# A two-layer hybrid trunk: the gate chain laid out on 32 rows, and retention tiles normalised in pairs

## The chip, the cores and the metric

The kernel runs on one core of a Trainium2 chip. The metric is the device time of one execution in microseconds (us); smaller is better. The kernel before was timed three times: 2268.85, 2267.9 and 2268.21 us, median 2268.21 us. A further execution was profiled: it took 2268.18 us, of which the recorded span of instructions is 2266.5 us.

## What is computed

Two layers run one after the other on x (1024 tokens by 1024 columns, f32). Each normalises x with gain and shift from a conditioning vector, multiplies by a wide input matrix, and cuts the result into two groups of four heads of 256 columns. The mLSTM heads have a short causal convolution, gates and a running maximum; the retention heads have rotary tables and a fixed decay. Both end in a per-head normalisation, a gate and an output product.

The part that the change touches first is the gate arithmetic of the mLSTM. Per head and token there are an input gate value `li` and a forget value `lf`:

```python
lf = log_sigmoid(f_pre)              # min(f, 0) - ln(1 + exp(-|f|))
b  = cumsum(lf)                      # over the tokens
u  = li - b
m  = running_max(u)                  # m0 = 0
# later: exp(u - m), exp(m_end - m), exp(-(b + m)), per token and head
```

The reference does it in chunks of 64; the kernel does it once over all 1024 tokens of 4 heads. Sums are kept in two pieces, a coarse one rounded to a grid (`bq`, from `lfq`) and a remainder (`br`), so that differences stay exact enough.

The second part is the retention group's per-head normalisation: for each tile of 128 tokens by 256 columns, subtract the mean and divide by the root of the variance plus a constant that depends on the place of the tile in its chunk.

## The kernel before, in words

**Matmuls.** Every f32 product is made of three matmuls of a high and a low half of each operand (`mm3`, lines 177 to 179, written `L177` to `L179` in the profile). A projection of one column block by 512 tokens is 24 such matmuls. Most projections are done in groups of seven products instead of eight (`pair_product` for q, k and z columns, `vpair_product` for the values of two heads), which costs additions on VectorE: of the token matrix once per layer (`build_forms`, L626 to L648) and of each weight block (`total`, L705).

**Order.** TensorE's order is the program's own (`tc.manual_schedule(engines={PE})`): a matmul that waits holds all matmuls behind it. The other engines' order is chosen by a planner that simulates the program; what is wrapped in `late(...)`, or called through the class `Later`, is pinned behind the instruction that was written just before it on its engine. All queues are in order on the chip, SyncE's (SP, which issues most DMAs) too.

**Ticks.** The side work is written as generators. `launch(gen, delay)` starts one, and `yield n` lets n ticks pass. A tick follows each unit of TensorE work: a quarter of a projection (12 matmuls of 128x512), or a slot. In the value products a slot is 24 matmuls of 128x256; a pair of heads takes 14 slots, in the order a12, a11, S2, S1, S3, a22, S4, two slots each. They write two kinds of PSUM tile: a12 pz, a11 px, S2 px, S1 pz, S3 px, a22 px, S4 pz. a22 adds to the bank that S3 wrote, so it has to wait until VectorE has read S3 (L824).

**The gate chain** (`gate_chain`, L503 to L590) is launched once per layer, when `gate_units` (L495) has put the gates of 1024 tokens into two PSUM tiles `pgs`, 4 rows of forget values (0 to 3) and 4 of input values (32 to 35), 512 tokens each. Around it run `build_forms` (in both layers), `rotary_tables` (layer 0 only) and the loading of the adaLN rows (`ada_rows`, L299, L307 and L309, and in layer 1 `gate_rows` with its product L345). The chain's own steps, for two halves of 512 tokens on 4 rows:

- tick 1: five ScalarE activations for each half (L516 to L519, L524)
- ticks 13 to 17, and 18 to 22 for the second half: fifteen VectorE instructions each, on 4 rows of 512, among them three scans (running sums and a running maximum, L535, L536, L548) that go on from the half before; four of them write into a 128-row tile `T4`. As V is `Later()`, the profile shows all of them as L144.
- tick 26: eight TensorE transposes of 128x128 (L562) turn the two `T4` into columns by token, copied to `COL`; then the exponentials for all heads. In layer 1, L345 follows on TensorE.

The chain's running maximum also goes to DRAM (`mdr`, L553), from where the attention reads it as rows. As working space the chain uses buffers that the attention owns later (`q`, `kc`, `dm`, `nd`, `cf`, `n`, `zt`, `cH`, `cL`).

**Retention normalisation.** `attention` runs per head by a table of steps. `values(j, tts)` makes the output tiles `tts` of chunk j; for retention heads it copies each to `nrm[j]` (one buffer, `n`) with L1144. Chunk 0 makes both tiles in one step; chunks 1 to 3 make them in two steps, some ticks apart, and each step launches a `normalise` of its own: statistics (L1160, L1161), variance plus constant (L1174), a power of minus one half on GpSimd (L1175, which writes `rsd`), minus mean times that (L1178, `nmu`), and the scaling on ScalarE (L1180). After the second tile, `finish` transposes the pair into `zt` (L1188) and stores it. That frees the buffer `n`.

Of the kernel before, what the change touches and what calls it, by code (L numbers as in the profile page):

```python
# [19 lines left out]
P = 128  # L20
# [67 lines left out]
def tile_hybrid_trunk(ctx, tc, x, xt, c, positions, w_ada, b_ada, norm_g, w_in, w_blk, w_val, conv_w, conv_b,  # L88
# [23 lines left out]
    def wt(tag, n, bufs, dt=F32):  # L112
        t = wrk.tile([P, 516 if tag == "acc" else n], dt, tag=tag, bufs=bufs, name=nm(tag))
        return t[:, 0:n] if tag == "acc" else t
# [91 lines left out]
           for l in range(DEPTH)]  # L206
    gbd = [dpool.tile([P, HALF], F32, name=f"gbd{i}") for i in range(2)]
    mdr = [dpool.tile([NH, T], F32, name=f"mdr{l}") for l in range(DEPTH)]

    ring = [cst.tile([P, 4 * 258], F32R, tag=f"ring{i}", name=f"ring{i}") for i in range(2)]  # L210
    ring3 = [r.rearrange("p (a c) -> p a c", a=4) for r in ring]
# [291 lines left out]
    def gate_chain(l, pgs, gt):  # L503
        V = Later()
        bg = cols[l][1]
        COL = wt("COL", 8 * 16, 1)
        C4 = COL.rearrange("p (t k h) -> p t k h", t=8, k=4)
        prev = {}
        on4 = ones.to_broadcast([P, 512])
        lfs, lis_, es = [], [], []  # L510
        mxs, fbs, lif = wt("q", 1024, 2), wt("q", 1024, 2), wt("kc", 1024, 1)
        for half in range(2):
            pg = pgs[half]
            hs = slice(half * HALF, (half + 1) * HALF)
            fb, li, e = fbs[:, hs], lif[:, hs], wt("dm", 512, 2)
            A.activation(fb[0:4], pg[0:4, :], AF.Identity, bias=bg[0:4, :])  # L516
            A.activation(li[32:36], pg[32:36, :], AF.Identity, bias=bg[32:36, :])
            A.activation(e[0:4], fb[0:4], AF.Abs)
            A.activation(e[0:4], e[0:4], AF.Exp, scale=-1.0)  # L519
            lfs.append(fb)  # L520
            lis_.append(li)
            es.append(e)
        for half in range(2):
            A.activation(es[half][0:4], es[half][0:4], AF.Ln, bias=ones[0:4, 0:1])  # L524
        yield 12
        T4s = []
        for half in range(2):
            lf, li, e = lfs[half], lis_[half], es[half]
            lfq = (wt("cf", 516, 1) if half else wt("nd", 516, 1))[:, 0:512]
            V.scalar_tensor_tensor(lf[0:4], lf[0:4], 0.0, e[0:4], ALU.min, ALU.subtract)  # L530
            V.tensor_scalar(lfq[0:4], lf[0:4], MAG_Q, -MAG_Q, ALU.add, ALU.add)
            V.tensor_tensor(lf[0:4], lf[0:4], lfq[0:4], ALU.subtract)
            bq, br = e, wt("zt", 512, 1) if half else wt("n", 512, 1)
            yield 1
            V.tensor_tensor_scan(bq[0:4], on4[0:4], lfq[0:4], prev.get("bq", 0.0), ALU.mult, ALU.add)  # L535
            V.tensor_tensor_scan(br[0:4], on4[0:4], lf[0:4], prev.get("br", 0.0), ALU.mult, ALU.add)  # L536
            yield 1
            lir, T4, mx = li, wt("cL" if half else "cH", 516, 1)[:, 0:512], mxs[:, half * HALF:(half + 1) * HALF]
            liq, uh = lf, lfq
            V.tensor_scalar(liq[0:4], li[32:36], MAG_Q, -MAG_Q, ALU.add, ALU.add)  # L540
            V.tensor_copy(lir[0:4], li[32:36])
            V.tensor_tensor(lir[0:4], lir[0:4], liq[0:4], ALU.subtract)
            G.memset(T4, 0.0)
            V.tensor_tensor(uh[0:4], liq[0:4], bq[0:4], ALU.subtract)
            yield 1
            V.tensor_copy(T4[0:4], uh[0:4])
            V.tensor_tensor(T4[32:36], lir[0:4], br[0:4], ALU.subtract)
            V.tensor_tensor_scan(mx[0:4], on4[0:4], uh[0:4], prev.get("mx", 0.0), ALU.mult, ALU.max)  # L548
            yield 1
            V.tensor_copy(T4[64:68], mx[0:4])  # L550
            V.tensor_tensor(uh[0:4], bq[0:4], mx[0:4], ALU.add)
            V.tensor_tensor(T4[96:100], uh[0:4], br[0:4], ALU.add)
            Q.dma_start(mdr[l][:, half * HALF:(half + 1) * HALF], mx[0:4])  # L553
            prev = {"bq": bq[0:4, 511:512], "br": br[0:4, 511:512], "mx": mx[0:4, 511:512]}
            T4s.append(T4)
            yield 1
        yield 3
        for half in range(2):
            T4 = T4s[half]
            pt = ps_a()  # L560
            for i in range(4):
                PE.transpose(pt[:, i * P:(i + 1) * P], T4[:, i * P:(i + 1) * P], ident)  # L562
            V.tensor_copy(C4[:, half * 4:(half + 1) * 4],
                          pt.rearrange("p (t k h) -> p t k h", t=4, k=4)[:, :, :, 0:4])
# [24 lines left out]
        V.tensor_tensor(we, we, eul4[:, :, 0:6, 0], ALU.mult)  # L589
        gt.update(C4=C4, eul4=eul4, em3=em3, wi=wi, we=we, dc=dc)  # L590
# [386 lines left out]
    def attention(l, hg, gt):  # L977
# [120 lines left out]
        def values(j, tts):  # L1098
# [6 lines left out]
            src = {}  # L1105
# [10 lines left out]
            for tt in tts:  # L1116
# [20 lines left out]
                if ml:  # L1137
                    if j > 0:
                        launch(gather(nd3[:, tt, 0:W], po[:, 0:W]), 1)
                    else:  # L1140
                        A.copy(nd3[:, tt, 0:W], po[:, 0:W])
                else:
                    src[tt] = nrm[j][:, tt, :]
                    A.copy(src[tt], po[:, 0:HD])  # L1144
# [10 lines left out]
        def normalise(j, tts, src):  # L1155
            n, a, b = len(tts), tts[0], tts[-1] + 1
            st6 = wt("st6", 12, 2)
            mv3 = wt("mv", 4, 2).rearrange("p (a b) -> p a b", a=2)
            for tt in tts:
                V.bn_stats(st6[:, 6 * tt:6 * tt + 6], src[tt])  # L1160
                V.bn_aggr(mv3[:, tt, :], st6[:, 6 * tt:6 * tt + 6])  # L1161
            va = wt("va", 2, 2)[:, 0:n]
            rs = wt("rsd", 2, 2)[:, 0:n]
            if ml:
                den = st["nd"][:, :, HD]
                r = wt("qd", 2, 2)
# [4 lines left out]
                G.tensor_tensor(rs, va, mhalf[:, 0:2], ALU.pow)  # L1171
            else:
                e = C_EPS + 2 * h + place(2 * j + a)
                V.tensor_tensor(va, mv3[:, a:b, 1], kc[:, e:e + n], ALU.add)  # L1174
                G.tensor_tensor(rs, va, mhalf[:, 0:n], ALU.pow)  # L1175
            yield 1
            nmu = wt("nmu", 2, 2)[:, 0:n]
            late(V.scalar_tensor_tensor(nmu, mv3[:, a:b, 0], -1.0, rs, ALU.mult, ALU.mult))  # L1178
            for i, tt in enumerate(tts):
                late(A.activation(nrm[j][:, tt, :], src[tt], AF.Identity, scale=rs[:, i:i + 1], bias=nmu[:, i:i + 1]))  # L1180
            if tts[-1] == 1:
                yield 1
                yield from finish(j)

        def finish(j):
            half = j // 2
# [530 lines left out]
```

## Time and profile before

| | |
|---|---|
| median of three runs | 2268.21 us |
| the profiled execution | 2268.18 us, span 2266.5 us |
| TensorE (PE) matmuls | 11483 |
| VectorE (DVE) busy | 1817.5 us |
| ScalarE (ACT) busy | 1159.4 us |
| GpSimd (POOL) busy | 964.3 us |

The profile gives times from the start of the span. A wait is idle time of an engine, put down to the instruction that ended it: `PE px L177 <- DVE acc L824` is TensorE waiting, at a matmul of line 177 that writes a px tile, for VectorE's instruction of line 824. `PEclk` is the share of TensorE's full clock that was granted. `SPq` is SyncE's queue. Rows of a timeline give start, duration, engine, line, operation and shape; merged neighbours carry a count.

### The profile page before, as it was taken

The page shows a single profiled execution, that of the slowest core. Times are in us where ns is not written, and L with a number is a line of the kernel's source. Part 1 is how long each engine was busy: PE and PEld are TensorE (multiplying, and loading weights), DVE is VectorE, ACT ScalarE, POOL GpSimd, SP SyncE. Part 2 cuts the span into 40 slices and gives each one's busy share as a digit, 9 for nine tenths or more (in the row PEclk, how much of TensorE's full clock was granted, in tenths as well). Part 3 has the DMA queues.
Part 4 walks back from the last instruction along what each step waited for, and adds up shares of the span by engine and source line. Part 5 has one row for each costly group of instructions (what it writes and reads, how often), then busy time and mean ns, then how long its engine had stood idle before and what let it go on. Part 6 is the DMA issues. An engine that isn't in the chain of part 4 may idle for free.

```text
span 2266.5 us, 35156 instructions
## 1 busy us (share of the span) xinstructions
PE 2151.5 (95%) x11483; PEld 1832.0 (81%) x11483; DVE 1817.5 (80%) x3205; ACT 1159.4 (51%) x2163; POOL 964.3 (43%) x842
## 2 busy tenths in 40 slices
PE   7988999999999999999999799999999899999998
PEld 5787789878898878788778678988987888788886
DVE  6899888989979998784738989788797889977653
ACT  7634345444565656553555434543565565655442
POOL 1443244445454454424366235544544453442313
PEclk9999999999999999999999899999999999999999
DMA  8266688787686777686633767776866686686974
GB/s 285 61 176 186 188 230 249 215 235 202 185 247 175 194 203 186 175 270 210 225 107 84 214 185 210 214 198 185 245 166 192 175 238 186 173 216 203 261 245 118
DMA packets 452549, 448.31 MB, mean 198 GB/s; under 512 B 191219, under 2 KB 309755, under 8 KB 452365
## 3 DMA queue, kind: packets, MB, share of 16 engines
q1 hardware_dynamic: 432636, 410.14, 58.9%
q0 software_dynamic: 19584, 35.66, 10.4%
q8 instruction: 90, 1.47, 0.3%
q14 instruction: 95, 0.77, 0.1%
q10 hardware_dynamic: 144, 0.26, 0.0%
HBM read 322.69 MB, written 123.24 MB: 197 GB/s over the span
## 4 chain that ended last, share of the span: by engine, by line
PE 57%; DVE 22%; DMA 10%; issue 5%; POOL 2%; ACT 2%; SPq 1%; DVEq 0%; POOLq 0%; ACTq 0%
PE px L177 8%; PE px L178 8%; PE px L179 8%; PE pz L179 6%; PE pz L178 6%; PE pz L177 6%; PE pa L177 4%; PE pa L179 4%; PE pa L178 4%; DVE acc L881 3%; DVE R L408 2%; PE pa L1123 2%; DVE acc L626 2%; DMA acc<-kfr 1%; PE pa L1032 1%
## 5 line engine op out<-in xcount | busy, mean ns | idle before, releaser
L403 ACT CAST wH<-R 128x512 fp32r<-128x512 f32 x616 | 377.2, 617 | 476.6 <-PE px L178 133.0
L408 POOL TENSOR_TENSOR R<-R,wH 128x512 fp32r<-128x512 f32 x276 | 397.5, 1447 | 479.5 <-ACT wH L403 325.9
L177 PE MATMUL px<-b,wH 128*128 128x512 f32 x912 | 364.8, 400 | 8.2 <-ACT acc L767 7.4
L179 PE MATMUL px<-b,R 128*128 128x512 f32 x912 | 365.7, 401 | 0.0
L178 PE MATMUL px<-b,wH 128*128 128x512 f32 x912 | 364.8, 400 | 0.0
L408 DVE TENSOR_TENSOR R<-R,wH 128x512 fp32r<-128x512 f32 x340 | 257.2, 760 | 90.5 <-ACT wH L403 87.5
L178 PE MATMUL pz<-b,wH 128*128 128x512 f32 x704 | 280.2, 398 | 1.3 <-DVE b L1262 1.3
L179 PE MATMUL pz<-b,R 128*128 128x512 f32 x704 | 281.0, 399 | 0.0
L177 PE MATMUL pz<-b,wH 128*128 128x512 f32 x704 | 279.8, 397 | 0.2 <-ACT acc L767 0.2
L177 PEld LDWEIGHTS px<-b,wH 128*128 128x128 f32 x912 | 174.6, 191 | 48.1 <-ACT acc L767 8.9
L179 PEld LDWEIGHTS px<-b,R 128*128 128x128 f32 x912 | 174.0, 191 | 42.0 <-POOL R L408 0.8
L178 PEld LDWEIGHTS px<-b,wH 128*128 128x128 f32 x912 | 174.4, 191 | 39.3
L177 PE MATMUL px<-wH,b 128*128 128x256 f32 (+1 forms) x576 | 177.7, 309 | 27.4 <-DVE acc L824 12.3
L178 PE MATMUL px<-R,b 128*128 128x256 f32 (+1 forms) x576 | 174.9, 304 | 3.7 <-DVE R L408 3.7
L179 PE MATMUL px<-wH,b 128*128 128x256 f32 (+1 forms) x576 | 175.8, 305 | 0.0
L701 POOL DMA_DIRECT2D R<-in_w_blk_dram x104 | 92.1, 886 | 185.3 <-DMA R<-in_w_blk_dram 90.8
L178 PEld LDWEIGHTS pz<-b,wH 128*128 128x128 f32 x704 | 133.5, 190 | 32.0 <-DVE b L1262 2.2
L179 PEld LDWEIGHTS pz<-b,R 128*128 128x128 f32 x704 | 133.3, 189 | 31.5
L177 PEld LDWEIGHTS pz<-b,wH 128*128 128x128 f32 x704 | 133.8, 190 | 29.4 <-ACT acc L767 0.6
L177 PEld LDWEIGHTS px<-wH,b 128*128 128x128 f32 x576 | 115.5, 201 | 32.2 <-ACT acc L817 10.4
L179 PE MATMUL pz<-wH,b 128*128 128x256 f32 (+1 forms) x448 | 134.0, 299 | 0.4 <-DVE b L1262 0.4
L177 PE MATMUL pz<-wH,b 128*128 128x256 f32 (+1 forms) x448 | 134.0, 299 | 0.0
(357 smaller groups left out, 5346.7 us busy)
## 6 DMA issues: line engine op xcount, KB each, us to landing
R<-in_w_blk_dram SPq DMA_DIRECT2D x276, 256.0 KB
vdr<-acc SPq DMA_DIRECT2D x128, 256.0 KB
ring<-vdr SPq DMA_DIRECT2D x64, 512.0 KB
R<-in_w_out_dram SPq DMA_DIRECT2D x128, 256.0 KB
R<-in_w_blk_dram POOLq DMA_DIRECT2D x104, 256.0 KB, 4.7
R<-in_w_val_dram SPq DMA_DIRECT2D x80, 256.0 KB
gdr<-acc SPq DMA_DIRECT2D x64, 256.0 KB
acc<-in_w_ada_dram SPq DMA_DIRECT2D x64, 256.0 KB
```

The lines of the kernel that those rows point to most:

```text
L177: PE.matmul(o, lt[0], rt[0], start=start, stop=False, skip_group_check=more)
L178: PE.matmul(o, lt[0], rt[1], start=False, stop=False, skip_group_check=more)
L179: PE.matmul(o, lt[1], rt[0], start=False, stop=stop, skip_group_check=more)
L403: A.copy(h, r)
L408: eng.tensor_tensor(lo, r, f(h), ALU.subtract)
L626: V.tensor_tensor(t, f(pair[0]), f(pair[1]), ALU.add)
L701: G.dma_start(raw[n], src, accum_op=ALU.add)
L881: V.scalar_tensor_tensor(acc[:, e:], pt[:, o + e - d:o + HALF - d], wcol, acc[:, e:], ALU.mult, ALU.add)
L1032: PE.matmul(pd, piece(kx[j], i, dt, tt * P, P), qd, start=dt == 0 and i == 0, stop=dt == 1 and i == 1)
L1123: PE.matmul(pi[:, 0:W], piece(qs[j], i, dt, tt * P, P), state[part][:, dt, 0:W], start=part + dt + i == 0, stop=ml and part + dt == 2)
```

## The change

**The gate chain** is written for 32 rows: row 8 h + t holds head h and the t-th block of 128 tokens.

- Tick 1: ScalarE adds the biases as before, into one tile `raw` (4 rows of 1024, twice), and two DMAs store it in DRAM (`gtd`, new). VectorE and GpSimd make three small constants.
- Tick 4: two DMAs read it back as 32 rows of 128. Tick 7: three activations.
- Tick 9: VectorE, seven instructions on 32x128, two of them scans that start anew in each row.
- Tick 12: two TensorE products with a 32x32 mask carry the sums of the earlier blocks of a head (`pc`); VectorE copies them, adds them, and scans the maximum in each row.
- Tick 15: TensorE transposes the 32 row ends into one row (`pm`); one VectorE scan over 32 numbers, with a zero at each head's start, carries the maximum.
- Tick 18: one TensorE product turns it back into a column (`pb`); VectorE finishes. Tick 20: one DMA to `mdr`.
- Tick 22: four transposes of 32x128 and one copy to `COL`; all that follows is as before.

**Retention**: `normalise` always takes both tiles of a chunk, and is launched after the second; one L1175, one L1174 and one L1178 in place of two.

```diff
+        raw = wt("kc", 1024, 1)
         for half in range(2):
+            for r in (0, 32):
+                A.activation(raw[r:r + 4, half * HALF:(half + 1) * HALF], pgs[half][r:r + 4, :], AF.Identity,
+                             bias=bg[r:r + 4, :])
+        for i in range(2):
+            Q.dma_start(gtd[l][i], raw[32 * i:32 * i + 4, :])
+        one, two = (wt("q", 1024, 2) for _ in range(2))
...
+        yield 3
+        for i, t in enumerate((fb, li)):
+            Q.dma_start(t, gtd[l][i].rearrange("h (b t) -> (h b) t", t=P))
+        yield 3
+        A.activation(e, fb, AF.Abs)
+        A.activation(e, e, AF.Exp, scale=-1.0)
+        A.activation(e, e, AF.Ln, bias=ones[0:32, 0:1])
+        yield 2
+        V.scalar_tensor_tensor(fb, fb, 0.0, e, ALU.min, ALU.subtract)
+        V.tensor_scalar(lfq, fb, MAG_Q, -MAG_Q, ALU.add, ALU.add)
+        V.tensor_tensor(fb, fb, lfq, ALU.subtract)
+        V.tensor_tensor_scan(bq, on, lfq, 0.0, ALU.mult, ALU.add)
+        V.tensor_tensor_scan(br, on, fb, 0.0, ALU.mult, ALU.add)
+        V.tensor_scalar(liq, li, MAG_Q, -MAG_Q, ALU.add, ALU.add)
+        V.tensor_tensor(lir, li, liq, ALU.subtract)
+        yield 3
+        pc = ps_a()
+        for i, b in enumerate((bq, br)):
+            PE.matmul(pc[0:32, i:i + 1], lower, b[:, P - 1:P], start=True, stop=True)
+        V.tensor_copy(carry[:, 0:2], pc[0:32, 0:2])
+        for i, b in enumerate((bq, br)):
+            V.tensor_scalar(b, b, carry[:, i:i + 1], None, ALU.add)
+        V.tensor_tensor(u, liq, bq, ALU.subtract)
+        V.tensor_tensor_scan(mx, on, u, 0.0, ALU.mult, ALU.max)
+        V.tensor_tensor(v, lir, br, ALU.subtract)
+        yield 3
+        pm = ps_a()
+        PE.transpose(pm[0:1, 0:32], mx[:, P - 1:P], ident[0:32, 0:32])
+        V.tensor_tensor_scan(inc[0:1], first[0:1], pm[0:1, 0:32], 0.0, ALU.mult, ALU.max)
+        V.tensor_tensor(exc[0:1, 1:32], inc[0:1, 0:31], first[0:1, 1:32], ALU.mult)
+        yield 3
+        pb = ps_a()
+        PE.matmul(pb[0:32, 0:1], exc[0:1, :], ones[0:1, 0:1], start=True, stop=True)
+        V.tensor_copy(carry[:, 2:3], pb[0:32, 0:1])
+        V.tensor_scalar(mx, mx, carry[:, 2:3], None, ALU.max)
+        V.tensor_tensor(s, bq, mx, ALU.add)
+        V.tensor_tensor(s, s, br, ALU.add)
+        yield 2
+        Q.dma_start(mdr[l].rearrange("h (b t) -> (h b) t", t=P), mx)
+        yield 2
+        pt = ps_a()
+        for i, t in enumerate((u, v, mx, s)):
+            PE.transpose(pt[:, i * 32:(i + 1) * 32], t, ident[0:32, 0:32])
+        V.tensor_copy(C4, pt[:, 0:P].rearrange("p (k h t) -> p t k h", k=4, h=4))
...
-            if not ml:
-                launch(normalise(j, tts, src), 1)
-            elif tts[-1] == 1:
-                launch(normalise(j, (0, 1), [nd3[:, tt, 0:HD] for tt in range(2)]), 1)
+            if tts[-1] == 1:
+                launch(normalise(j, [nrm[j][:, tt, 0:HD] for tt in range(2)]), 1)
```

More of the change, by code (lines that the diff above doesn't have):

```diff
@@ L208, in tile_hybrid_trunk @@
     mdr = [dpool.tile([NH, T], F32, name=f"mdr{l}") for l in range(DEPTH)]
+    gtd = [dpool.tile([2, NH, T], F32, name=f"gtd{l}") for l in range(DEPTH)]
     ring = [cst.tile([P, 4 * 258], F32R, tag=f"ring{i}", name=f"ring{i}") for i in range(2)]
@@ L523, in gate_chain @@
[L523 to L556, printed above, removed]
@@ L557, in gate_chain @@
-        yield 3
[L558 to L564, printed above, removed]
+            for r in (0, 32):
+                A.activation(raw[r:r + 4, half * HALF:(half + 1) * HALF], pgs[half][r:r + 4, :], AF.Identity,
+                             bias=bg[r:r + 4, :])
@@ new lines, in gate_chain @@
+        for i in range(2):
+            Q.dma_start(gtd[l][i], raw[32 * i:32 * i + 4, :])
+        one, two = (wt("q", 1024, 2) for _ in range(2))
+        e, bq, br, fb, lfq, lir, tmp, small = (one[0:32, i * P:(i + 1) * P] for i in range(8))
+        u, v, mx, s, li, liq = (two[0:32, i * P:(i + 1) * P] for i in range(6))
+        lower, inc, exc, first = (small[:, i * 32:(i + 1) * 32] for i in range(4))
+        carry = two[0:32, 6 * P:6 * P + 4]
+        on = ones[0:32].to_broadcast([32, P])
@@ new lines, in gate_chain @@
+        G.memset(lower, 1.0)
+        l3 = lower.rearrange("p (h t) -> p h t", h=4)
+        G.affine_select(l3, l3, [[-8, 4], [0, 8]], ALU.is_ge, 0.0, base=0, channel_multiplier=1)
+        G.affine_select(lower, lower, [[1, 32]], ALU.is_ge, 0.0, base=-1, channel_multiplier=-1)
+        nc.vector.memset(first, 1.0)
+        nc.vector.memset(first.rearrange("p (h t) -> p h t", h=4)[:, :, 0:1], 0.0)
+        nc.vector.memset(exc, 0.0)
+        yield 3
+        for i, t in enumerate((fb, li)):
+            Q.dma_start(t, gtd[l][i].rearrange("h (b t) -> (h b) t", t=P))
@@ L1104, in values @@
             nd3 = st["nd"]
-            src = {}
             ahead = {}
@@ L1142, in values @@
                 else:
-                    src[tt] = nrm[j][:, tt, :]
-                    A.copy(src[tt], po[:, 0:HD])
-            if not ml:
-                launch(normalise(j, tts, src), 1)
-            elif tts[-1] == 1:
-                launch(normalise(j, (0, 1), [nd3[:, tt, 0:HD] for tt in range(2)]), 1)
+                    A.copy(nrm[j][:, tt, :], po[:, 0:HD])
+            if tts[-1] == 1:
+                launch(normalise(j, [nrm[j][:, tt, 0:HD] for tt in range(2)]), 1)
         def gather(nd, po):
@@ L1153, in gather, with normalise @@
             yield
-        def normalise(j, tts, src):
-            n, a, b = len(tts), tts[0], tts[-1] + 1
+        def normalise(j, src):
             st6 = wt("st6", 12, 2)
             mv3 = wt("mv", 4, 2).rearrange("p (a b) -> p a b", a=2)
-            for tt in tts:
+            for tt in range(2):
                 V.bn_stats(st6[:, 6 * tt:6 * tt + 6], src[tt])
                 V.bn_aggr(mv3[:, tt, :], st6[:, 6 * tt:6 * tt + 6])
-            va = wt("va", 2, 2)[:, 0:n]
-            rs = wt("rsd", 2, 2)[:, 0:n]
+            va = wt("va", 2, 2)
+            rs = wt("rsd", 2, 2)
             if ml:
@@ L1170, in normalise @@
                 V.tensor_tensor(va, va, mv3[:, :, 1], ALU.add)
-                G.tensor_tensor(rs, va, mhalf[:, 0:2], ALU.pow)
             else:
-                e = C_EPS + 2 * h + place(2 * j + a)
-                V.tensor_tensor(va, mv3[:, a:b, 1], kc[:, e:e + n], ALU.add)
-                G.tensor_tensor(rs, va, mhalf[:, 0:n], ALU.pow)
-            yield 1
[L1177 to L1183, printed above, removed]
+                e = C_EPS + 2 * h
+                if j in WHOLE:
+                    V.tensor_tensor(va, mv3[:, :, 1], kc[:, e:e + 2], ALU.add)
+                else:
+                    V.tensor_scalar(va, mv3[:, :, 1], kc[:, e:e + 1], None, ALU.add)
+            G.tensor_tensor(rs, va, mhalf[:, 0:2], ALU.pow)
+            yield 1
+            nmu = wt("nmu", 2, 2)
+            late(V.scalar_tensor_tensor(nmu, mv3[:, :, 0], -1.0, rs, ALU.mult, ALU.mult))
+            for tt in range(2):
+                late(A.activation(nrm[j][:, tt, :], src[tt], AF.Identity, scale=rs[:, tt:tt + 1], bias=nmu[:, tt:tt + 1]))
+            yield 1
+            yield from finish(j)
         def finish(j):
```

14 lines of the change are left out of this document (removed).

## The prediction

> **What bounds the kernel now.** I read the page first, then TensorE's waits in the two stretches where the gate chain runs, then what each engine does there.
>
> ```profile
> span 2266.5 us, 35156 instructions
> PE 2151.5 (95%) x11483; PEld 1832.0 (81%) x11483; DVE 1817.5 (80%) x3205; ACT 1159.4 (51%) x2163; POOL 964.3 (43%) x842
> ```
>
> TensorE is busy 95% of the span, so 115 us of idle time is all that an edit of other engines can win, less what its clock loses after a wait. Which waits the chain can touch is told by TensorE's waits from 60 to 260 us (layer 0) and from 1190 to 1320 us (layer 1): us in total, times, longest.
>
> ```profile
> PE px L177 <- DVE acc L824: 7.4, 1, 7.4
> PE px L177 <- ACT acc L767: 5.4, 1, 5.4
> PE pa L562 <- DVE cL L144: 4.4, 1, 4.4
> PE px L177 <- ACT acc L817: 2.1, 2, 1.1
> ```
>
> ```profile
> PE px L177 <- DVE acc L824: 4.9, 1, 4.9
> PE pa L345 <- ACT wH L868: 4.0, 1, 4.0
> PE pa L562 <- DVE cL L144: 3.0, 1, 3.0
> ```
>
> The chain's transposes L562 wait in both layers for VectorE. Who is late is told by the busy times (PE, PEld, DVE, ACT, POOL, each with its count; then PEclk) of a window of each layer, and by those of line 144 alone in the second:
>
> ```profile
> 134.00:180.00 46.00, 38.78 (x294) 37.78 (x294) 45.60 (x76) 15.72 (x28) 18.83 (x11) 0.91 0.65 166
> 1257.00:1304.00 47.00, 39.27 (x202) 33.36 (x202) 43.39 (x71) 22.55 (x35) 9.93 (x8) 0.86 0.74 212
> ```
>
> ```profile
> 1257.00:1304.00 47.00, 24.50 (x40) 0.86 0.74 212
> ```
>
> VectorE is busy 45.60 of 46 us in layer 0 and 43.39 of 47 in layer 1, and in layer 1 24.50 us of that are the chain. So in these stretches **VectorE is the limit and TensorE waits for it**. A wait costs more than itself:
>
> ```profile
> 134.00:138.00 4.00, 4.00 (x20) 0.50 0.68 253
> 145.00:149.00 4.00, 4.00 (x35) 1.00 0.40 55
> 1305.00:1309.00 4.00, 3.96 (x13) 0.74 0.69 128
> 1312.00:1316.00 4.00, 4.00 (x19) 1.00 0.94 254
> ```
>
> After the wait of 7.4 us the granted clock is 0.50 for 4 us and 20 matmuls pass where later 35 do: 4 x 15/35 = 1.7 us lost. After those of layer 1 it is 0.74, and 13 pass for 19: 1.3 us. From 35 in 4 us, a slot of 24 matmuls takes 2.8 us.
>
> **The chain's VectorE time.** Line 144 in the layer 1 window is the chain's halves and some ten small instructions that stay (1.6 us at 0.16, below); with the chain's first, ahead of the window, the halves take 24.5 - 1.6 + 0.7 = 23.6 us. The new instructions have 128 elements in a row, not 512:
>
> ```profile
> L144 DVE TENSOR_SCALAR acc<-acc x48: 273/290/1269, 127.3 to 228.8; 128x256 f32<-128x256 f32 x48
> L144 DVE TENSOR_TENSOR acc<-acc x12: 404/424/1399, 128.6 to 224.8; 128x256 f32<-128x256 f32 x12
> L144 DVE TENSOR_TENSOR_SCAN dm<-ones,nd x2: 1200/1202/1203, 136.7 to 1258.8; 4x512 f32<-4x512 f32 x2
> L1178 DVE SCALAR_TENSOR_TENSOR nmu<-mv,rsd x88: 110/160/1274, 320.5 to 2095.6; 128x1 f32<-128x1 f32 x48, 128x2 f32<-128x2 f32 x40
> ```
>
> Between a 256-wide instruction (0.29 with one tensor, 0.42 with two) and a 1 or 2-wide one (0.16), 128 wide is about 0.2 and 0.3; a scan, 1.2 for 512, about 0.4. Seven of 0.3, five of 0.2, three scans, the copy to COL (0.25) and seven tiny ones of 0.16 make 5.7 us a layer. If width did not count at all, the bounds are 23 x 0.16 = 3.7 us and, at the 256-wide and 512-wide prices, some 10. I take 5.7, so **18 us less VectorE work in each layer** (14 to 20).
>
> **What that removes from TensorE.** With VectorE no longer full after the first waits, I strike L562 in both layers (4.4 + 1.7 and 3.0 us); in layer 0 the short ones of L817 (2.1); in layer 1 L345, which gets its data from an addition (L338, then the split L868) that VectorE did right behind the chain's last copy: 4.0 + 1.3. Together 8.2 and 8.3 us.
>
> ```profile
> 1298.89 0.68 DVE L338 TENSOR_TENSOR acc<-acc,acc 1x512 f32<-1x512 f32 x1 [0.21 <-DVE COL L144]
> ```
>
> The waits for L824 lie before the chain's first VectorE instruction (133.85 in layer 0, below; in layer 1 it comes after L824 too) and are not among them. The new transposes and products on TensorE, eight small ones, stand for eight of 128x128: nothing either way.
>
> **What it adds: waits in TensorE's own order.** The chain now has matmuls at ticks 12, 15 and 18 too, and whatever is not ready holds all matmuls behind it. Where tick 12 lies is seen from the change of bank, from pz (S1, slots 7 and 8) to px (S3), in TensorE's order; when VectorE gets to the chain's instructions of tick 9, from `build_forms` L647, which is written just before them; and what a22 then waits for is L824:
>
> ```profile
> 120.23 0.28 PE L179 MATMUL pz<-wH,b 128*128 128x256 f32 x1
> 1245.64 0.29 PE L179 MATMUL pz<-wH,b 128*128 128x256 f32 x1
> ```
>
> ```profile
> 120.60 1.28 DVE L647 SCALAR_TENSOR_TENSOR acc<-acc,acc 128x512 f32<-128x512 f32 x2
> 132.92 0.68 DVE L824 TENSOR_TENSOR acc<-px,acc 128x512 f32<-128x512 f32 x1
> 133.85 0.67 DVE L144 SCALAR_TENSOR_TENSOR q<-q,dm 4x512 f32<-4x512 f32 x1
> 1249.35 1.28 DVE L647 SCALAR_TENSOR_TENSOR acc<-acc,acc 128x512 f32<-128x512 f32 x2
> 1255.80 0.68 DVE L824 TENSOR_TENSOR acc<-px,acc 128x512 f32<-128x512 f32 x1
> ```
>
> TensorE comes to `pc` at 120.3 and 1245.8. VectorE begins the block at about 121.9 and 1250.6; the five instructions up to the second scan take 1.6 us, with others between them I say 3, so the carries' inputs are there at 124.9 and 1253.6. **TensorE waits 4.6 and 7.9 us at `pc`**, then runs at half clock. But this is not all added: VectorE goes on during it, and the L824 waits shrink. In layer 0 TensorE reaches a22 at 124.9 + 2 slots + 1.7 = 132.2; L824 ended at 133.6, which let a22 go on, and has 3 us of chain work ahead of it now: a22 goes on at 136.6, 3.0 us later. In layer 1 it reaches a22 at 1260.9, when L824 (1256.5 + 3) is done: 4.4 us later than before, less the 1.7 us of half clock that followed there: 2.7. Sum of both: **+5.7 us** (bounds: 0, if the block floats ahead of `build_forms`; 16, the two waits and half clocks whole).
>
> At `pm` and `pb` I charge nothing: between ticks 12 and 18 TensorE needs 6 slots, 17 us, and VectorE has nine small chain instructions and a load that no longer fills it. [...]
>
> **ScalarE and the queues.** The round trip through DRAM is new: two stores, two loads, and one `mdr` store for two. Behind them in SP's queue stand weight loads and gate stores, and SP does get stuck:
>
> ```profile
> 99.31 7.38 SPq L601 DMA_DIRECT2D gdr<-acc  x2
> SPq L601 <- DVE acc L600: 26.4, 4, 12.9
> 676.49 6.27 DMA dm<-mdr
> L524 ACT ACT_TABLE_LOAD  x4: 1283/1283/1283, 80.5 to 1214.0; - x4
> L517 ACT ACTIVATE kc<-pa,bg x4: 679/681/684, 78.5 to 1209.7; 4x512 f32<-4x512 f32 x4
> ```
>
> SP held gate stores for VectorE four times, 12.9 us at the longest, and two of them until 106.7. Should the loads of `fb` and `li` stand behind those, they are issued at 107; with 6.3 us, the long load of such rows in the chain of waits, three ScalarE instructions of under 0.7 and two table loads of 1.28 the block is ready at 118, 4 us before VectorE reaches it (121.9). Nothing, as long as VectorE is that late; if it came earlier, `pc` would wait for the loads instead. The `mdr` store stands in SP's queue waiting for VectorE as it did before, with weight loads behind it. ScalarE, 15.72 of 46 us busy, has three instructions for six longer ones; GpSimd three small ones for two.
>
> **Downstream.** The wait for L767 near 230 us (5.4 + 1.7 half clock) is ScalarE waiting for a buffer that VectorE's L307 frees, behind the rotary tables, whose work the old chain delayed.
>
> ```profile
> ACT acc L767 <- DVE acc L307: 3.2, 1, 3.2
> ```
>
> With 18 us less ahead of it I take half: -3.5 (0 to -7).
>
> **Retention pairs.** Three chunks of four heads in two layers: 24 pairs.
>
> ```profile
> L1175 POOL TENSOR_TENSOR rsd<-va,mhalf 128x1 f32<-128x1 f32 x48 | 37.1, 773 | 35.6 <-DVE va L1174 33.3 <-PE px L179 1.1 <-ACT wH L403 0.2
> L1175 POOL TENSOR_TENSOR rsd<-va,mhalf 128x2 f32<-128x2 f32 x8 | 6.6, 826 | 17.6 <-DVE va L1174 15.8 <-DMA R<-in_w_blk_dram 1.7
>   DVE zt L1188: 12.1, 6
>   PE pa L177: 4.6, 1
> L1180 ACT ACTIVATE n<-n,nmu,rsd x64: 583/602/618, 322.7 to 1716.8; 128x256 f32<-128x256 f32 x64
> ```
>
> GpSimd saves 48 x 0.773 - 24 x 0.826 = 17 us, VectorE 48 x 0.16 = 8, none of it on TensorE's path: GpSimd is 43% busy. Against it, the first tile's scaling (0.6) now follows the second's statistics, so the transposition that frees `n` is 0.6 us later, and the next L1144 with it. The second and third rows are what L1144 waited for and who waited for it: the transposition held it six times, and TensorE waited for it once, 4.6 us. I take -1 (bounds -5, that one wait gone, to +4, six times 0.6). [...]
>
> **Sum.** -8.2 - 8.3 + 5.7 - 3.5 - 1.0 = -15.3, from 2268.2 (the profiled execution, 2268.18, is at the median): **2253 us**. The planner orders everything anew behind the change; an estimate for that is 4 us either way, one wait like those of 4.0 to 4.9 us above coming or going.
>
> **Rivals.**
> - *More is freed* (15%): the L767 wait goes whole (-3.5 more) and the block is taken earlier, so `pc` costs 2: 2268 - 16.5 + 2 - 7 - 1 = 2246. For it: VectorE is the limit. Against: L647 stands ahead.
> - *Given back* (17%): the tables' and buffers' next limit is a DMA in SP's queue, so L767 stays, and the `pc` waits cost 12: 2268 - 16.5 + 12 - 1 = 2263. For it: SP's stall of 7 us above.
> - *Slower, by TensorE's queue* (13%): VectorE's lag outlasts the three slots (8.4 us) between `pc`, `pm` and `pb`. Before, the instruction of tick 13 ran at 133.85 where TensorE had passed it at 123.1 (120.3 + 2.8): a lag of 10.8. If the lag stays so, each of the four waits costs 2.4 + up to 1.7, with `pc` whole (16): 2268 - 16.5 + 16 + 16 - 1 = 2283, no gain downstream. It decides where VectorE's lag at ticks 12 and 15 is over 8.4 us. Against it: the lag of 10.8 was built up by `build_forms`, which ends there, and TensorE's own wait at `pc` takes it away.
>
> **The numbers.** Forecast 55%, its own range 2245 to 2261. The range for 8 in 10 takes in most of the first rival and the second: 2242 to 2268. A change under 0.2% (4.5 us) can't be told from none here. Faster by more 78%, within 10%, slower 12%.
>
> **What would show it.** Right: line 144 (chain) near 6 us a layer; no wait at the last transposes and L345; a wait at `pc` of 4 to 8 us and a smaller one for L824; none at `pm` and `pb`. Wrong: waits at all three; VectorE still full from 137 to 180; a wait of ScalarE for the loads of `fb` that holds its evacuations; or a gain in retention that exceeds that of the chain.

## The result, and the profile after

The changed kernel takes **2247.2 us** (median of 4 runs, 2239.2 to 2249.7) against 2268.1 for the kernel before beside it: ratio 0.9904, interval 0.988 to 0.9928, so 16 to 27 us less. The forecast was 2253. Executions of one kernel spread by up to some 20 us, so every comparison below is by ratio and interval; multiplied by 2268, a ratio step of 0.001 is 2.3 us. The profiled execution took 2247.5 us. Lines of the changed kernel stand one to eight further down: 767, 817, 824 and 345 are now 775, 825, 832 and 346; 408 is 409; the transposes 562 are 571; `pc` is 547, `pm` 556, `pb` 561.

The page's span and first part:

```profile
span 2245.8 us, 35049 instructions
PE 2140.3 (95%) x11489; PEld 1824.9 (81%) x11489; DVE 1779.4 (79%) x3139; ACT 1142.2 (51%) x2151; POOL 940.7 (42%) x820
```

VectorE has 38 us less, GpSimd 24. Of the 20.7 us between the two spans only 9.5 are idle time of TensorE (span less busy, 115.0 to 105.5); the other 11.2 are busy time, as nearly the same matmuls pass at a mean granted clock of 0.986 for 0.979. So in these two traces about half of the gain is clock. TensorE's waits from 60 to 260 us, then from 1170 to 1320 us:

```profile
PE px L178 <- DVE R L409: 5.4, 1, 5.4
PE pa L556 <- DVE q L144: 3.0, 1, 3.0
PE px L177 <- ACT acc L775: 2.9, 1, 2.9
PE pa L547 <- DVE q L144: 2.9, 1, 2.9
PE px L177 <- DVE acc L832: 1.3, 1, 1.3
```

```profile
PE pa L547 <- DVE q L144: 10.2, 2, 9.1
PE px L178 <- DVE R L409: 2.4, 2, 2.0
```

Gone are the waits at the last transposes in both layers, the one for line 346 in layer 1, and nearly all for line 832. In their place stand `pc` in both layers (2.9 and 10.2 us), `pm` in layer 0 and, not foreseen, line 409. The engines in the same stretches as before (the second moved with layer 1, which starts 14 us earlier), and then the tile `q`, which holds the new chain from tick 9 on but for its last copy to `COL` (0.28 us a layer), in four windows:

```profile
134.00:180.00 46.00, 43.04 (x345) 42.47 (x344) 41.23 (x103) 17.61 (x32) 13.05 (x12) 0.96 0.83 227
1242.00:1289.00 47.00, 47.00 (x266) 41.19 (x267) 30.68 (x61) 20.37 (x36) 12.40 (x10) 0.95 0.75 206
```

```profile
123.00:145.00 22.00, 0.70 (x5) 0.42 (x5) 6.75 (x15) 0.00 (x0) 0.00 (x0) 0.82 0.54 184
145.00:180.00 35.00, 0.65 (x6) 0.45 (x6) 0.95 (x4) 0.00 (x0) 0.00 (x0) 0.97 0.85 219
1235.00:1245.00 10.00, 0.52 (x4) 0.35 (x4) 6.18 (x13) 0.00 (x0) 0.00 (x0) 0.56 1.00 308
1245.00:1290.00 45.00, 0.83 (x7) 0.53 (x7) 1.33 (x6) 0.00 (x0) 0.00 (x0) 0.98 0.73 198
```

In the first window TensorE passes 345 matmuls for 294 and its clock is 0.96 for 0.91; in the second 266 for 202 and 0.95 for 0.86. The second comparison flatters the change: both windows of layer 1 begin right behind a wait, of 4.9 us for line 824 before and of 10.2 us at `pc` now. By the table below, layer 1 is only 3.4 us better at line 346 (-14.2 to -17.6). The chain takes VectorE 7.7 us in layer 0 (6.75 + 0.95) and 7.5 in layer 1. The prediction counted 23.6 for the old one; its rows sum to 26.3 us in layer 0 and 23.9 in layer 1, so 18 and 16 us are taken away.

Where TensorE stands against before, from the first matmul of the same group in each trace (us; negative is earlier):

| | gates' product, layer 0 | 252 us before: first sum of the adaptive part | 650 us before: first product of 258 columns | gates' product, layer 1 | line 346 (345 before, at 1302 us) | last matmul |
|---|---|---|---|---|---|---|
| changed kernel | +0.1 | -8.5 | -14.8 | -14.2 | -17.6 | -20.3 |
| without data at `pc` | +0.4 | -7.8 | -14.3 | -12.9 | -19.5 | -25.4 |
| load in layer 0 | +0.5 | +4.1 | +2.7 | +4.3 | +1.2 | -6.0 |
| load in layer 1 | -0.2 | -7.8 | -11.9 | -10.6 | -9.1 | -15.2 |

The first row is the result by place: -8.5 in the chain's own stretch of layer 0, -6.3 in the 400 us behind it, -6.1 in layer 1. The other rows are of the experiments below. They are single executions, and one kernel's differ by several us, so only steps of more than 3 us are read from them.

### The profile page after: what moved, and what is told of

Same layout as the page of the kernel before. It is cut to its first block, busy times and chain, and to the rows that moved or that the text cites. A ratio compares the mean times of both kernels' runs of the same rounds, so it can differ in the third digit from the quotient of the medians.

```text
span 2245.8 us, 35049 instructions
## 1 busy us (share of the span) xinstructions
PE 2140.3 (95%) x11489; PEld 1824.9 (81%) x11489; DVE 1779.4 (79%) x3139; ACT 1142.2 (51%) x2151; POOL 940.7 (42%) x820
## 3 DMA queue, kind: packets, MB, share of 16 engines
q0 software_dynamic: 19584, 35.66, 10.4%
## 4 chain that ended last, share of the span: by engine, by line
PE 54%; DVE 21%; DMA 12%; issue 6%; ACT 3%; POOL 2%; SPq 2%; DVEq 0%; POOLq 0%; ACTq 0%
PE px L177 7%; PE px L178 7%; PE px L179 7%; PE pz L178 6%; PE pz L179 5%; PE pz L177 5%; PE pa L177 4%; PE pa L179 4%; PE pa L178 4%; DMA R<-in_w_blk_dram 3%; DVE acc L889 2%; DVE R L409 2%; PE pa L1130 2%; DMA acc<-kfr 1%; DVE acc L634 1%
## 5 line engine op out<-in xcount | busy, mean ns | idle before, releaser
L178 PE MATMUL pz<-R,b 128*128 128x256 f32 (+1 forms) x448 | 132.9, 297 | 0.0
```

The costliest lines, as they stand in the source:

```text
L178: PE.matmul(o, lt[0], rt[1], start=False, stop=False, skip_group_check=more)
```

## The experiments

**Theory:** VectorE is the limit where the chain runs, and the change gains by taking 16 to 18 us a layer from it; the waits at `pc` and `pm` give part of it back. **Rivals:** the gain comes from the pairs; or from where the chain's transposes, DMAs and waits stand in the order, whatever VectorE has to do. All times are medians with the ratio to the kernel before and its interval.

### The two halves of the change

`e1_gate_only` has the new `gate_chain` and the old retention; `e2_pairs_only` the old chain and the new retention. Each is the diff above cut in two.

> The new gate chain alone; retention tiles are normalised one at a time as before. Theory A (the gate chain gives all but what the prediction charged for the pairs, 1 us): 2248, with the whole difference to the changed kernel within 1 us. Rival B (the 5.8 us that TensorE wins between 240 and 1183 us of the changed kernel come from the pairs in layer 0): about 2253. Rival C (pairs and chain only work together, through the planner's order): above 2258.

> The old gate chain; only the retention tiles are normalised two at a time. Theory A: 2267 (1 us less than before). Rival B: 2262, with TensorE's waits between 240 and 1183 us some 5.8 us shorter than before. Rival D (the first tile's later scaling costs more than the instructions saved): 2270 to 2272.

Measured: the chain alone 2249.6 (0.9922, 0.9905 to 0.9939), the pairs alone 2263.5 (0.9973, 0.996 to 0.9986). So the chain is worth 14 to 22 us and the pairs 3 to 9, more than the 1 us that the forecast gave them; together they agree with the whole change (18 + 6 against 22). Rival C falls, the parts add up. Rival B falls too as it was put: without the pairs TensorE wins 4.4 us between 252 and 650 us all the same (-6.0 to -10.4 in the trace of the chain alone).

Where the pairs win is not to be seen. The prediction tied one wait to them, that of 4.6 us for the tile `n`. In TensorE's waits over the whole run it is now, in the changed kernel, with the chain alone and with the pairs alone:

```profile
PE pa L177 <- ACT n L1150: 3.0, 1, 3.0
```

```profile
PE pa L177 <- ACT n L1152: 2.4, 1, 2.4
```

```profile
PE pa L177 <- ACT n L1142: 3.5, 1, 3.5
```

It is shorter in all three, and shortest without the pairs, so the pairs can't be named as what shortens it. The pairs' trace was taken in an execution of 2270.1 us, the longest of its 12, and TensorE is idle in it for 123.8 us, longer than before (115.0). That the pairs gain is measured; by what is open.

### VectorE's load taken out without the new order, and put back into it

`e6_old_short` keeps the old chain, its order and its transposes, and narrows its VectorE instructions:

```diff
-            V.tensor_tensor_scan(bq[0:4], on4[0:4], lfq[0:4], prev.get("bq", 0.0), ALU.mult, ALU.add)
+            V.tensor_tensor_scan(bq[0:4, W], on4[0:4, W], lfq[0:4, W], prev.get("bq", 0.0), ALU.mult, ALU.add)
...
```

(with `W = slice(0, 128)`, and so on for all of them; it leaves out three quarters of the chain, its old instructions then sum to 9.3 and 10.4 us in the two layers for 26.3 and 23.9, and GpSimd gets one small memset more.) `e5_vector_load` is the changed kernel with:

```diff
+            for i in range(10):
+                yield 1
+                D.tensor_tensor_scan(y[0:4], ones.to_broadcast([P, 512])[0:4], x[0:4], 0.0, ALU.mult, ALU.add)
+                D.tensor_tensor(x[0:4], x[0:4], x[0:4], ALU.mult)
         launch(gate_chain(l, pgs, gt), 1)
+        launch(load_vector(), 12)
```

> The old chain in its old order, with its last transposes as before, but each of its VectorE instructions works on 128 of its 512 columns, and what it passes on is zero: it leaves out three quarters of the chain, so only its time means anything. Old work 23.6 us a layer; at 128 wide some 30 instructions of about 0.25 make 8 us. If VectorE's load in those stretches is what TensorE waited for: the waits at the last transposes, at line 345 and most of that for 767 go, with no waits at pc and pm in their place: 2268 - 16.5 - 4 = 2247 or less, at or below the gate chain alone. If the gain needs the new order (short steps spread over ticks 9 to 22): 2260 or more.

> The changed kernel, with 19 us of VectorE work per layer put back that nothing uses: ten times a scan and an addition-like instruction of 4x512 at ticks 13 to 22, where the old chain stood (1.2 + 0.67 us each). If relief of VectorE is the cause: most of the 16.5 us comes back, and pm and pb, which now stand behind that work, wait as well: 2262 to 2275. If the gain comes from where the chain's transposes and DMAs stand and not from VectorE's time: within 3 us of the changed kernel, 2250.

Measured: 2249.5 (0.9919, 0.989 to 0.9948) with the short old chain, 2267.2 (1.0009, 0.9993 to 1.0025) with the load. The first wins as much as the new chain alone (0.9922) with none of its order, the second loses the whole gain with all of its order. (The load sums to 22.8 us in layer 0 and 19.8 in layer 1, somewhat more than was taken away; in the trace TensorE waits for none of its tiles.) **VectorE's time is the cause**; the rival of the order falls. The clock goes along: over all executions its median is 0.981 before, 0.984 with the chain alone, 0.985 with the short old chain and 0.980 with the load. TensorE's waits with the load, 60 to 260 us and 1170 to 1320 us:

```profile
PE pa L556 <- DVE q L144: 6.4, 1, 6.4
PE px L178 <- DVE R L409: 5.4, 1, 5.4
PE px L177 <- DVE acc L832: 4.8, 2, 4.1
PE pa L547 <- DVE q L144: 2.6, 1, 2.6
```

```profile
PE pa L547 <- DVE q L144: 10.2, 1, 10.2
PE pa L346 <- ACT wH L876: 4.1, 1, 4.1
```

`pm` waits 6.4 us for 3.0, line 832 is back at 4.8, and the wait of line 346, 4.0 before the change, stands again at 4.1.

### The load by layer

`e11_load_l0` and `e12_load_l1` put the same load into one layer:

```diff
+        if l == 0:
+            launch(load_vector(), 12)
```

> The changed kernel with the 19 us of unused VectorE work in layer 0 alone. The prediction had layer 0 at -8.7 (waits, pc and downstream) and layer 1 at -5.6; the traces show about -14 by the start of layer 1 and -6 in it. With both layers loaded all 20 us were lost. If the -14 is layer 0's relief: 2259 to 2262. If the stretch from 250 to 1183 us won its 6 us by another cause (the pairs, the planner's order): 2253 to 2256.

> The same load in layer 1 alone. By the traces: 2247 + 6 = 2253. If layer 1's relief is worth more, through what follows it: 2256 to 2259; if the two layers together make less than the run with both: the loss is not a sum over layers.

Measured: 2257.8 (0.9947, 0.9929 to 0.9964) with layer 0 loaded, 2255.5 (0.9946, 0.9923 to 0.9968) with layer 1: each costs about 10 us of the 22 (0.0043 and 0.0042), 20 together, where both at once cost 24 (0.0105). By the intervals each of the two costs is known to some 7 us, so they agree with an equal share and do not prove one; both times lie between the two forecasts. The table shows where, in single executions: with layer 0 loaded TensorE wins 1.4 us between 252 and 650 us (+4.1 to +2.7), without the load 6.3. That points to layer 0's relief as what the stretch behind the chain gains by; by which instructions is not shown. With layer 1 loaded, line 346 comes 1.5 us later against the layer's start (-10.6 to -9.1), where the changed kernel comes 3.4 earlier: 4.9 us lost there, with the wait of 4.1 us for line 876 back. The rest of that row's distance (-10.6 for -14.2) arose ahead of layer 1, where the two kernels have the same instructions, so I put it down to the spread of executions.

### What the wait at `pc` costs

`e7_pc_no_data` takes away what `pc` waits for; `e3_pc_later` moves it; `e4_block_early` moves VectorE's instructions ahead of it; `e8_early_late` does both.

```diff
-            PE.matmul(pc[0:32, i:i + 1], lower, b[:, P - 1:P], start=True, stop=True)
+            PE.matmul(pc[0:32, i:i + 1], lower, ones[0:32, 0:1], start=True, stop=True)
```

```diff
-        yield 3
+        yield 6
         pc = ps_a()
```

In `e4_block_early` the `yield 2` ahead of VectorE's block goes and the `yield 3` ahead of `pc` becomes `yield 5`; in `e8_early_late` the second is `yield 7`. `e7_pc_no_data` leaves out the true carries, so only its time counts.

> The changed kernel, but the products at pc multiply a column of ones in place of the last column of the scans, so that they wait for nothing of VectorE's; the carries are wrong, all else is done. It prices the wait at pc. Theory A of the prediction (the wait is partly given back, as VectorE works on during it and the wait for line 832 shrinks; net 3 us in layer 0 and 2.7 in layer 1): 2241 to 2243, with a wait for line 832 of 4 to 7 us back in layer 1. Rival B (the waits at pc are paid whole, 2.9 and 9.1 + 1.1 us and the half clock): 2233 to 2235. Rival C (the wait only changes its place): 2247.

> pc three slots later (tick 15 for 12), and all that follows it too; nothing else. TensorE gets to pc 8.4 us later, so the waits of 2.9 and most of 9.1 us at pc go, that at pm too. Theory A: as in the run without data at pc, a wait for line 832 takes the place in layer 1, net gain 4 to 6 us: 2241 to 2243. Rival C: 2247. Rival D: the later columns make the attention of the first head wait for the chain: 2250 or more.

> VectorE's first seven instructions of the chain two ticks earlier (7 for 9), ahead of the second half of build_forms; pc stays at tick 12. If VectorE's backlog at pc is what TensorE waits for, any place in the queue ahead of build_forms does: pc's wait in layer 1 falls from 9.1 to under 2, and the backlog of build_forms delays line 832 by the 3 us of the block: 2241 to 2244. If the planner's order cancels it: 2247.

> Both: the block at tick 7 and pc at tick 14. No wait at pc, pm, pb or the last transposes in either layer; what is left of the two stretches is the wait for line 832, at 3 to 5 us each: 2239 to 2243. If that wait takes all, 2247.

| | median us | ratio | interval |
|---|---|---|---|
| changed kernel | 2247.2 | 0.9904 | 0.988 to 0.9928 |
| no data at `pc` | 2242.8 | 0.9893 | 0.9871 to 0.9915 |
| `pc` three slots later | 2238.0 | 0.9861 | 0.9835 to 0.9887 |
| block two ticks earlier | 2241.1 | 0.9879 | 0.9856 to 0.9902 |
| both, `pc` two slots later | 2243.9 | 0.9886 | 0.986 to 0.9913 |

Without data at `pc` TensorE's waits are, 60 to 260 us and 1170 to 1320 us:

```profile
PE px L177 <- DVE acc L832: 8.0, 2, 5.1
PE px L178 <- DVE R L409: 5.4, 1, 5.4
```

```profile
PE px L177 <- DVE acc L832: 7.1, 1, 7.1
PE px L178 <- DVE R L409: 2.0, 1, 2.0
```

So 13.1 us of waits at `pc` (2.9 + 10.2) and 2.4 at `pm` (3.0 to 0.6) give way to 13.8 more for line 832 (8.0 + 7.1 - 1.3). The wait mostly changes its name; VectorE has the same backlog whether TensorE stands at `pc` or at the next bank. What is left is 2 to 5 us (by ratio 2.5, by median 4.4), which the intervals do not tell from nothing; by the table it is 3.2 in layer 1, where line 346 comes 6.6 us earlier against the layer's start (-12.9 to -19.5) and 3.4 in the changed kernel, and nothing in layer 0. Of the expectations, theory A (2241 to 2243) fits best, B (12 us or more) falls, and C (2247, nothing gained) is not excluded by this run. With the block two ticks earlier, the same stretch of layer 1 has no wait at `pc` but another name again, GpSimd's part of the splits (line 832 is 831 there):

```profile
PE px L178 <- POOL R L409: 5.2, 1, 5.2
PE px L178 <- DVE R L409: 2.4, 2, 2.0
PE px L177 <- DVE acc L831: 1.8, 1, 1.8
```

With `pc` three slots later nothing waits at `pc` or `pm`, and line 832 holds TensorE for 9.7 us in layer 0 and 7.0 in layer 1. Summed over both stretches, TensorE's waits are 28.8 us in the changed kernel and 23.8 to 25.2 in the four versions. All four medians lie below the changed kernel's. That of `pc` later is the lowest, below the 2241 to 2243 expected of it; the intervals overlap, that of `pc` later barely. Against the kernel before each is faster, its interval wholly below 1.

### Line 409, and the version that the runs point to

In layer 0 the changed kernel has a wait of 5.4 us that ends at 106.98 and was 1.5 before (1.9 with a second one just behind it). GpSimd, then VectorE there, in the kernel before and in the changed one:

```profile
102.34 5.16 POOL L869 TENSOR_TENSOR b<-acc,b 128x512 fp32r<-128x512 f32 x3 [0.47 <-ACT b L868]
```

```profile
102.24 0.68 DVE L408 TENSOR_TENSOR R<-R,wH 128x512 fp32r<-128x512 f32 x1
```

```profile
101.75 0.89 POOL L709 DMA_DIRECT2D R<-in_w_val_dram  x1
102.36 4.00 POOL L877 TENSOR_TENSOR b<-acc,b 128x512 fp32r<-128x512 f32 x3
```

```profile
102.27 4.65 DVE L409 TENSOR_TENSOR R<-R,wH 128x512 fp32r<-128x512 f32 x1
```

The subtraction takes 4.65 us for 0.68: it ends 0.6 us after three additions of GpSimd in a row, which take 4.00 us for the 5.16 before. `e9_pool_phase` puts the old chain's two memsets back ahead of them, and `e10_best` does that and moves `pc`:

```diff
+        for tag in ("cH", "cL"):
+            G.memset(wt(tag, 516, 1)[:, 0:512], 0.0)
```

> The changed kernel, with the old chain's two GpSimd memsets of 128x512 put back (0.52 us each, near 86 us in layer 0); nothing uses them. In the changed kernel and in every run with the new chain, VectorE's line 409 at 102.27 us takes 4.65 us for 0.68, just as long as three GpSimd additions in a row (102.36 to 106.4), and TensorE waits 5.4 us for it; before, it began 0.1 us ahead of GpSimd and took 0.68. Theory: that is a matter of about 0.1 us between the two engines, and 1 us more of GpSimd work ahead of it takes the wait back to 1.5: 4 to 5 us faster, 2242 to 2243. Rival: the wait comes from the chain itself (its DMAs or ScalarE steps), and stays: 2247 to 2248.

> The changed kernel with pc three slots later and the two GpSimd memsets: the version that the runs so far point to. If both gains stand by themselves: 2238 - 4 = 2234. If the memsets change nothing: 2238. If the wait for line 832 in layer 0 takes what line 409 gives back: 2238 too, with that wait 4 us longer than 6.5.

Measured: 2249.1 (0.9914, 0.9892 to 0.9935) and 2246.0 (0.9891, 0.987 to 0.9911). The wait stays (5.5 us in both), as the rival said; that the chain's own DMAs or ScalarE steps cause it is not shown. With the memsets, GpSimd and VectorE:

```profile
101.50 0.91 POOL L711 DMA_DIRECT2D R<-in_w_val_dram  x1
102.11 4.02 POOL L879 TENSOR_TENSOR b<-acc,b 128x512 fp32r<-128x512 f32 x3
```

```profile
102.03 4.66 DVE L409 TENSOR_TENSOR R<-R,wH 128x512 fp32r<-128x512 f32 x1
```

The two memsets were absorbed by a shorter pause of GpSimd before it came to this place, and the three additions start in the same position to VectorE's again, so the run does not test the theory of the 0.1 us by moving them. The rows do speak against it: VectorE starts 0.10 us ahead of GpSimd before (102.24, 102.34) and 0.09 after. TensorE's wait for the subtraction is 5.4 us in the traces of the changed kernel, of the chain alone, with the load in both layers, without data at `pc` and with `pc` later, and nowhere longer than 1.8 in those of the kernel before and of the pairs alone. That the subtraction lasts until GpSimd has done its three additions is in the rows; why it takes 4.65 us beside them, when the three instructions of that shape that VectorE ran beside GpSimd's three in the kernel before (from 102.96 on) took 1.67, 1.78 and 1.79, stays open. A DMA that GpSimd issues until 102.64 overlaps its start, and before the change that DMA (100.99 to 101.87) ended 0.37 us ahead of the subtraction, and GpSimd was idle for 0.47 us in between; that was not tried as a cause. The fastest version measured is `pc` three slots later without the memsets; `e10_best`, which differs by the memsets alone, is 8 us slower by median, with intervals that overlap (up to 0.9887, from 0.987), so for that move the runs support a time between 2238 and 2246.

## Why the prediction was right, and where its steps missed

The sign, the mechanism and the size of the chain hold: 2253 forecast, 2247.2 measured. That the total came as near as 6 us is in part luck, as several terms missed both ways. By its steps:

- **VectorE is the limit there**: right, shown by both directions (short old chain, load put back). In layer 0 it still is nearly: 41.23 of 46 us are busy after the change, so "still full from 137 to 180", named as a sign of being wrong, came in part.
- **The chain's VectorE time, 5.7 us a layer**: 7.7 and 7.5, and 0.3 for the copy to `COL`, inside the bounds of 3.7 to 10; of the 18 us less, 18 and 16 came. The excess is in instructions that ran beside GpSimd's. The chain's instructions by kind (duration min, median, max in ns), then the block in layer 1:

```profile
L144 DVE TENSOR_TENSOR q<-q x8: 173/267/1250, 125.1 to 1255.0; 32x128 f32<-32x128 f32 x6, 1x31 f32<-1x31 f32 x2
L144 DVE TENSOR_SCALAR q<-q x6: 190/237/1273, 123.8 to 1264.2; 32x128 f32<-32x128 f32 x6
L144 DVE TENSOR_TENSOR_SCAN q<-ones,q x6: 386/906/1472, 126.3 to 1243.3; 32x128 f32<-32x128 f32 x6
```

```profile
1237.34 0.21 DVE L144 TENSOR_SCALAR q<-q 32x128 f32<-32x128 f32 x1
1237.58 1.24 DVE L144 TENSOR_TENSOR q<-q 32x128 f32<-32x128 f32 x1
1238.74 2.81 DVE L144 TENSOR_TENSOR_SCAN q<-ones,q 32x128 f32<-32x128 f32 x2
...
1243.29 0.40 DVE L144 TENSOR_TENSOR_SCAN q<-ones,q 32x128 f32<-32x128 f32 x1
```

  The interpolated 0.2, 0.3 and 0.4 are what these shapes take while GpSimd is idle, from 1241.3 on (0.19, 0.28, 0.40); beside GpSimd the addition takes 1.24 and the two scans 1.4 each. GpSimd at that time:

```profile
1236.69 3.25 POOL L877 TENSOR_TENSOR b<-acc,b 128x512 fp32r<-128x512 f32 x2 [2.29 <-ACT b L876]
1239.90 1.37 POOL L409 TENSOR_TENSOR R<-R,wH 128x512 fp32r<-128x512 f32 x1
```

  That is 1.0 us more for a 32x128 instruction, as much as for a 128x512 one beside GpSimd in the kernel before (1.67 to 1.79 for 0.68). One TENSOR_SCALAR, with a single tensor, took 1.27 us as well (at 123.80, GpSimd adding from 123.70 on), and another, also beside GpSimd, 0.21 (at 1237.34, above).
- **The waits struck out** (last transposes, line 345, the short ones of 817): gone, as predicted.
- **`pc`: 4.6 and 7.9 us predicted, 2.9 and 10.2 measured.** In layer 0 TensorE came 4.4 us later than reckoned, held by line 409; in layer 1 the addition and the two scans beside GpSimd made the block 5.6 us long (1235.87 to 1241.5) where I had put 3. That most of it takes the place of the wait for line 824 was right: +5.7 net was predicted, 2 to 5 measured, not told from nothing by the intervals.
- **`pm` charged at nothing: failed in layer 0**, 3.0 us. The claim was that a load that no longer fills VectorE would be done in time. Up to 145 us it still fills it:

```profile
123.00:145.00 22.00, 16.09 (x108) 15.54 (x108) 21.16 (x50) 7.23 (x13) 6.84 (x6) 0.82 0.54 184
```

  The rotary tables, which the chain used to hold up, now run among its steps: the copy that takes `pc`'s result comes 10 us after `pc` (127.81), behind 5.9 us of theirs (line 144 with `acc`) and 4 us of other work:

```profile
137.89 0.42 DVE L144 TENSOR_TENSOR acc<-acc,acc 128x256 f32<-128x256 f32 x1
138.24 0.14 DVE L144 COPY q<-pa 32x2 f32<-32x2 f32 x1
```

  In layer 1, which has no tables, `pm` waits for nothing. This is the "slower" rival's mechanism, at one place of four and at 3.0 us; with the load back it is 6.4.
- **Half clock after a wait**: right at `pc` (0.50 in both layers, behind waits of 2.9 and of 9.1 + 1.1 us). Whether a wait of under 3 us costs clock has an answer in the runs: at times (0.50 behind 2.9 us at `pc`, 1.00 behind 2.9 us for line 775; last section). But the sum reckoned clock only behind the waits that it named, 1.3 to 1.7 us each, and 11.2 of the 20.7 us between the two traces are faster matmuls; not all of that is traced to single waits.
- **The round trip through DRAM, hidden**: right. ScalarE, then VectorE, on the loaded rows:

```profile
87.57 0.31 ACT L533 ACTIVATE q<-q 32x128 f32<-32x128 f32 x1 [0.31 <-DMA q<-gtd]
```

```profile
123.50 0.27 DVE L144 SCALAR_TENSOR_TENSOR q<-q 32x128 f32<-32x128 f32 x1
```

  The rows are there 36 us before VectorE turns to them.
- **Downstream -3.5: too small.** The wait for line 767 fell from 5.4 to 2.9, about the half that was taken; but TensorE wins another 6.3 us between 252 and 650 us, 2.6 of them shorter waits and 3.7 faster matmuls, which no step held. With the load in layer 0 only 1.4 are left, which points to the same relief, further on, in single executions.
- **The pairs -1, bounds -5 to +4: mis-sized**, -3 to -9 measured, by a path that no trace shows.

The terms that missed cancel in part: line 409 (+3.5, 5.4 for 1.9) and `pm` (+3.0), each with some lost clock, against downstream (-6.3 more) and the pairs (-2 to -8 more). Of the rivals, "more is freed" (2246) lies nearest in time and in kind; its first half, the whole wait for line 767, did not come.

## What to carry to other kernels

A serial stretch of small instructions on the engine that bounds a stage is worth a good part of its own time, and not all of it in the stretch itself: here 16 to 18 us off VectorE in a layer moved the end by about 10. When a step is split over TensorE's queue, ask of each new wait which old wait behind it shrinks; only the difference is a cost, and three slots (8.4 us) between producer and product were not enough while that engine had 10 us of other work in line. Put a load back to test a claim of relief: it is cheap, and it tells relief from rearrangement.

## What the runs showed of the hardware

**A wait of about 3 us costs the clock in one place or trace and not in another.** The four microseconds behind waits of 2.9 (at `pc`), 3.0 (`pm`) and 2.9 (for line 775) in the changed kernel, with the clock in the third column from the end:

```profile
127.80:131.80 4.00, 3.93 (x20) 3.83 (x21) 3.97 (x11) 0.00 (x0) 0.00 (x0) 0.50 0.38 126
142.60:146.60 4.00, 4.00 (x24) 3.96 (x25) 3.62 (x14) 0.62 (x1) 1.73 (x2) 0.68 0.56 159
223.90:227.90 4.00, 3.96 (x17) 3.24 (x18) 3.02 (x6) 3.10 (x6) 1.55 (x1) 1.00 1.06 323
```

and behind one wait for line 832 (834), at the same place, without data at `pc` (2.83 us) and in `e10_best` (2.85 us):

```profile
185.30:189.30 4.00, 4.00 (x19) 4.00 (x20) 3.86 (x10) 2.20 (x4) 0.88 (x1) 0.50 0.41 71
```

```profile
184.00:188.00 4.00, 4.00 (x33) 4.00 (x34) 3.86 (x10) 2.83 (x5) 0.00 (x0) 1.00 0.54 73
```

19 matmuls pass in one, 33 in the other: 1.7 us from a wait of the same length. What decides between the two, the rows do not show. Such waits may be part of why executions of one kernel differ by 10 us and more; that is argued, not tested.

**A VectorE instruction took 4.65 us for 0.68 beside three GpSimd additions in a row**, and 4.66 in `e9_pool_phase`. By the trace of the changed kernel it began first (102.27 against 102.36), and it ended 0.6 us after the last of the three. In the kernel before, the same subtraction began 0.10 us ahead of three such additions and took 0.68; the three VectorE instructions that followed beside them took 1.67 to 1.79 each. What decides between the two, no run shows.
